# The MLPs' down product: pairs of 256 hidden columns multiplied two at a time in seven products

## The chip, the cores and the metric

One core of a Trainium2 chip runs the whole program in one launch. The metric is the device time of one execution in microseconds. The kernel before took 2644.26 us, the median of three runs (2640.12 to 2646.15).

## What is computed

A trunk of two layers over a sequence of 1024 positions with 1024 channels, in float32. Each layer has a token mixer (a Mamba-2 mixer in layer 0, a gated short convolution in layer 1) and then an MLP. Each sub-layer normalises, scales and shifts by a condition c, and is added back with a gate. The change is in the MLP, where h is 1024 x 1024, `up_w` 1024 x 4096 and `down_w` 4096 x 1024:

```python
def sqrelu_mlp(h, up_w, down_w):
    a = jax.nn.relu(h @ up_w)
    return (a * a) @ down_w
...
        x = x + g_f * sqrelu_mlp(h, mlp_up[i], mlp_down[i])
```

## The kernel before

Activations are kept transposed: `xT[(dt, hf)]` holds 128 channels (dt of 8) by 512 positions (half hf of 2), so a matmul takes 128 x 128 weights and gives 128 x 512 in one PSUM bank. For precision each operand is split in two: a weight tile into hi (cast on ScalarE), lo (raw minus hi, on VectorE) and a bf16 copy (ScalarE), by `split3` (L776), and an activation into ah and al by `keep` (L830). One product of two 128-wide blocks is then three matmuls, hi x ah, lo x ah and bf16 x al, which `mul` (L810) issues into one bank.

`mlp` (L1068) goes over the 4096 hidden columns in 16 pairs of 256. `part_a` and `part_b` (L1016, L1030) make the four blocks of a pair's up product (two blocks of 128 columns by two halves of positions) by seven products of half size (Winograd's form): two in `part_a`, giving c11, and five in `part_b`, giving c12, c22 and c21. In `part_b` GpSimd makes four sums of raw weights (L1036 to L1039) and two of the sums of results (L1052, L1065), and VectorE evicts the other banks (L1050, L1055, L1059, L1063). `relu2` (L1073, its instruction on L1074) squares the ReLU on VectorE. `keep` stores each block in rings of buffers, three for c11 and six for the others.

`do_d` (L1085) is the down product of one pair, by `second` (L840): for each of two halves of the 1024 output channels it loads a raw tile of 512 KB, splits it, and for each of four output tiles and each half of positions runs `mul` over the pair's two blocks, six matmuls into one of four banks tagged "sp". VectorE evicts each bank with the gate into x (L870). A pair is 84 matmuls up and 96 down.

The first two pairs are done apart (`plain_a`, `plain_b`), while the combinations of h are still being made by `combos` (L881) on VectorE, ScalarE and GpSimd. The steady loop then goes, for each i, `do_b(i + 1)`, `do_d(i)`, `do_a(i + 3)`. The last two pairs go through `second` together, with the next stage's work behind each tile.

In layer 0 the down product carries background work: `ada` (L145) makes layer 1's modulation in 48 steps of one 512 KB load and two multiply-adds on VectorE (L160, L162). `do_d` calls one or two steps in each half of the output channels. Raw weights of every kind, ada's among them, share three tiles ("wraw"); hi, lo and bf16 weights have two buffers each.

The order on each engine is made at build time by a scheduler that goes by program order, readiness and priorities; weight splits and GpSimd's sums carry a raised priority. Each engine then runs its own instructions strictly in that order. SyncE issues nearly all loads; GpSimd issues eight small parameter loads at the start (L101 to L116).

## Time and profile before

| | |
|---|---|
| median of three runs | 2644.26 us |
| the profiled execution | 2639.07 us, of which span 2637.4 us |
| TensorE clock granted, mean | 0.98 of full speed |
| busy: TensorE / VectorE / ScalarE / GpSimd | 95% / 77% / 46% / 23% |
| matmuls | 11498 |
| layer 0's MLP, layer 1's MLP | about 860 to 1515 us, 1980 to 2637 us |

An engine counts as busy while an instruction of it is open, also while that instruction itself is held up. A matmul's own duration overlaps the next one's, so their pace is read from counts over a stretch and not from their means.

### The profile page before, as it was taken

The page shows a single profiled execution, that of the slowest core. Times are in us where ns is not written, and L with a number is a line of the kernel's source. Part 1 is how long each engine was busy: PE and PEld are TensorE (multiplying, and loading weights), DVE is VectorE, ACT ScalarE, POOL GpSimd, SP SyncE. Part 2 cuts the span into 40 slices and gives each one's busy share as a digit, 9 for nine tenths or more (in the row PEclk, how much of TensorE's full clock was granted, in tenths as well). Part 3 has the DMA queues.
Part 4 walks back from the last instruction along what each step waited for, and adds up shares of the span by engine and source line. Part 5 has one row for each costly group of instructions (what it writes and reads, how often), then busy time and mean ns, then how long its engine had stood idle before and what let it go on. Part 6 is the DMA issues. An engine that isn't in the chain of part 4 may idle for free. (4 is left out here: it accounts for less than half of the span.)

```text
span 2637.4 us, 31558 instructions
## 1 busy us (share of the span) xinstructions
PE 2503.7 (95%) x11498; PEld 1742.9 (66%) x11498; DVE 2040.8 (77%) x3084; ACT 1226.3 (46%) x2258; POOL 594.3 (23%) x465
## 2 busy tenths in 40 slices
PE   7999999999998799999999998999988999999998
PEld 5777777777776456666666654666544666666666
DVE  7887798887888987878777679765798666666666
ACT  3685565675574524333433345534453343333434
POOL 4221120121121422122222103332234211122120
PEclk9899999999999999999999999999999999999999
DMA  7644443445442233333334122222221221222221
GB/s 226 178 132 132 122 130 107 135 126 150 136 125 61 65 102 105 113 119 111 114 102 120 56 61 75 73 64 70 67 64 48 64 66 55 72 65 64 72 63 74
DMA packets 332412, 256.26 MB, mean 97 GB/s; under 512 B 8824, under 2 KB 289104, under 8 KB 332256
## 3 DMA queue, kind: packets, MB, share of 16 engines
q1 hardware_dynamic: 332000, 254.12, 32.5%
q8 instruction: 90, 1.47, 0.2%
q14 instruction: 66, 0.54, 0.1%
q0 software_dynamic: 256, 0.12, 0.1%
HBM read 249.75 MB, written 4.46 MB: 96 GB/s over the span
## 5 line engine op out<-in xcount | busy, mean ns | idle before, releaser
L870 DVE SCALAR_TENSOR_TENSOR x<-mm,mod,x 128x512 f32<-128x512 f32 (+1 forms) x536 | 387.3, 739 | 136.4 <-PE mm L826 135.2
L826 PEld LDWEIGHTS <-wbf 128*128 128x128 bf16 x2268 | 192.3, 98 | 343.0 <-issue 195.2
L826 PE MATMUL mm<-hh,whi 128*128 128x512 f32 x1196 | 369.0, 427 | 22.5 <-ACT whi L783 9.0
L826 PE MATMUL mm<-ah,wlo 128*128 128x512 f32 (+1 forms) x1072 | 389.9, 427 | 0.0
L826 PE MATMUL mm<-ah,whi 128*128 128x512 f32 (+1 forms) x1072 | 364.4, 431 | 18.5 <-DVE x L870 14.6
L826 PE MATMUL mm<-hh,wlo 128*128 128x512 f32 x1196 | 370.4, 416 | 10.9 <-DVE wlo L784 10.8
L826 PE MATMUL mm<-hl,wbf 128*128 128x512 bf16 x1196 | 318.2, 385 | 4.3 <-ACT wbf L785 4.3
L826 PE MATMUL mm<-al,wbf 128*128 128x512 bf16 (+1 forms) x1072 | 311.6, 382 | 3.7 <-DVE x L870 3.5
L826 PEld LDWEIGHTS mm<-hh,whi 128*128 128x128 f32 x1196 | 230.3, 193 | 71.9 <-ACT hh L956 12.8
L826 PEld LDWEIGHTS mm<-hh,wlo 128*128 128x128 f32 x1196 | 226.9, 190 | 70.2 <-DVE wlo L784 15.7
L208 PE MATMUL mm<-hh,whi 128*128 128x512 f32 x616 | 248.6, 404 | 0.7 <-ACT xs L556 0.7
L210 PE MATMUL mm<-hl,whi 128*128 128x512 f32 x616 | 246.0, 399 | 0.0
L209 PE MATMUL mm<-hh,wlo 128*128 128x512 f32 x616 | 245.4, 398 | 0.3 <-DVE wlo L194 0.3
L826 PEld LDWEIGHTS mm<-ah,whi 128*128 128x128 f32 x1072 | 204.0, 191 | 58.8 <-DVE x L870 17.8
L826 PEld LDWEIGHTS mm<-ah,wlo 128*128 128x128 f32 x1072 | 204.1, 190 | 52.9 <-issue 0.3
L784 DVE TENSOR_TENSOR wlo<-wraw,whi 128x1024 fp32r<-128x1024 f32 x139 | 177.3, 1285 | 66.8 <-ACT whi L783 66.4
L783 ACT CAST whi<-wraw 128x1024 fp32r<-128x1024 f32 x139 | 144.1, 1047 | 129.6 <-PE mm L826 116.3
L785 ACT CAST wbf<-wraw 128x1024 bf16<-128x1024 f32 x139 | 143.7, 1043 | 120.5 <-PE mm L826 116.4
L1036 POOL TENSOR_TENSOR ws<-wraw 128x512 f32<-128x512 f32 x37 | 50.4, 1361 | 493.8 <-DMA wraw<-in_mlp_up_dram 474.5
L208 PEld LDWEIGHTS mm<-hh,whi 128*128 128x128 f32 x616 | 116.5, 189 | 30.6 <-issue 5.8
L210 PEld LDWEIGHTS mm<-hl,whi 128*128 128x128 f32 x616 | 116.5, 189 | 27.3 <-issue 3.7
L209 PEld LDWEIGHTS mm<-hh,wlo 128*128 128x128 f32 x616 | 116.5, 189 | 27.0 <-issue 3.5
(390 smaller groups left out, 4410.6 us busy)
## 6 DMA issues: line engine op xcount, KB each, us to landing
wraw<-in_mlp_up_dram SPq DMA_DIRECT2D x100, 512.0 KB, 3.9
adaw<-in_ada_w_dram SPq DMA_DIRECT2D x96, 512.0 KB, 4.4
wraw<-in_ssd_in_w_dram SPq DMA_DIRECT2D x82, 512.0 KB, 3.9
wdraw<-in_mlp_down_dram SPq DMA_DIRECT2D x64, 512.0 KB, 3.6
wraw<-in_sc_in_w_dram SPq DMA_DIRECT2D x39, 512.0 KB, 3.6
L<-da SPq DMA_DIRECT2D x32, 512.0 KB, 5.0
wdraw<-in_ssd_out_w_dram SPq DMA_DIRECT2D x32, 512.0 KB, 3.4
E<-de SPq DMA_DIRECT2D x56, 128.0 KB, 4.5
```

Source lines behind the costliest of these rows:

```text
L208: PE.matmul(ps, lhsT=hi[:, o:o + P], rhs=ah, start=(k == 0), stop=False)
L209: PE.matmul(ps, lhsT=lo[:, o:o + P], rhs=ah, start=False, stop=False)
L210: PE.matmul(ps, lhsT=hi[:, o:o + P], rhs=al_, start=False, stop=(k == nk - 1))
L783: A.copy(hi[:, :w], raw)
L784: V.tensor_tensor(out=lo[:, :w], in0=raw, in1=hi[:, :w].bitcast(F32), op=ALU.subtract)
L785: A.copy(b[:, :w], raw)
L826: PE.matmul(ps, lhsT=at((hi, lo, b)[j], offs[i]), rhs=blocks[i][j // 2], start=(e == 0), stop=(e == len(js) - 1))
L870: V.scalar_tensor_tensor(out=xv, in0=ps, scalar=g, in1=xv, op0=ALU.mult, op1=ALU.add)
L1036: PL.tensor_tensor(out=s1, in0=a21, in1=a22, op=ALU.add)
```

## The change

Twelve of the sixteen pairs of each MLP (2 to 13) are taken two at a time: their up products, then one `do_w` for both. `do_w` makes the down product of the two pairs for one half of the output channels from seven products, each for two output tiles with two blocks of 128 hidden columns. The seven activation operands of each pair (four blocks and the combinations T1 to T4) are made and kept in `do_b`. Three of the products go through the banks Z: ScalarE reads the bank with the gate applied, GpSimd adds that to x, and the next product is summed into the same bank (`mul` with start=False). The other four end in an eviction by VectorE. Rings of kept activations become one of 14 buffers. To make room in SBUF the program's scratch for GpSimd's own loads is cut to 1024 bytes, and the eight parameter loads at the start go from GpSimd's queue to ScalarE's. The last two pairs and the first two stay as they are.

```diff
-    PL.dma_start(sb[0:96], ssd_conv_w[0].rearrange("k (r p) -> (k r) p", p=P))
+    A.dma_start(sb[0:96], ssd_conv_w[0].rearrange("k (r p) -> (k r) p", p=P))
...
+    def split_to(dst, o, src, pri=200):
+        hi, lo, b = [t[:, o:o + 512].rearrange("p (i n) -> p i n", i=2) for t in dst]
+        with tc.high_priority(offset=pri):
+            A.copy(hi, src)
+            V.tensor_tensor(out=lo, in0=src, in1=hi.bitcast(F32), op=ALU.subtract)
+            A.copy(b, src)
...
-    def keep(tag, r):
-        ah = mp.tile([P, TH], F32R, tag=tag + "h", name=nm("ah"), bufs=dict(a1=3, ab=6)[tag])
-        al_ = mp.tile([P, TH], BF16, tag=tag + "l", name=nm("al"), bufs=dict(a1=3, ab=6)[tag])
+    def keep(r):
+        ah = mp.tile([P, TH], F32R, tag="abh", name=nm("ah"), bufs=14)
+        al_ = mp.tile([P, TH], BF16, tag="abl", name=nm("al"), bufs=14)
...
         def do_a(i):
             c, m1s[i] = part_a(mlp_up[l], i * 256, H)
-            aa[i] = [[keep("a1", relu2(c)), None], [None, None]]
+            cs[i] = relu2(c)
 
         def do_b(i):
-            for (f, hf), c in zip(((0, 1), (1, 1), (1, 0)), part_b(mlp_up[l], i * 256, H, m1s.pop(i))):
-                aa[i][f][hf] = keep("ab", relu2(c))
+            c11 = cs.pop(i)
+            c12, c22, c21 = [relu2(c) for c in part_b(mlp_up[l], i * 256, H, m1s.pop(i))]
+            if i >= n - 2:
+                aa[i] = [[keep(c11), keep(c12)], [keep(c21), keep(c22)]]
+                return
+            b = dict(B11=keep(c11))
+            PL.tensor_tensor(out=c11, in0=c12, in1=c11, op=ALU.subtract)
+            b["B22"] = keep(c22)
+            PL.tensor_tensor(out=c12, in0=c22, in1=c12, op=ALU.subtract)
+            V.tensor_tensor(out=c22, in0=c22, in1=c11, op=ALU.subtract)
+            b["B21"] = keep(c21)
+            V.tensor_tensor(out=c21, in0=c21, in1=c22, op=ALU.subtract)
+            b.update(T1=keep(c11), T2=keep(c22), T3=keep(c12), T4=keep(c21))
+            aa[i] = b
...
+        def do_w(i):
+            ba, bb = aa.pop(i), aa.pop(i + 1)
+            B = {k: [ba[k], bb[k]] for k in ba}
+            w = mlp_down[l]
+            for ds in range(2):
+                raw = [wp.tile([P, 1024], F32, tag="wraw", name=nm("wdraw"), bufs=3) for _ in range(2)]
+                for e in range(2):
+                    SY.dma_start(raw[e].rearrange("p (k n) -> p k n", k=4),
+                                 w[i * 256:i * 256 + 512, ds * 512 + e * 256:ds * 512 + e * 256 + 256].rearrange("(k p) n -> p k n", p=P))
+                (a11, a12), (a21, a22) = [[t.rearrange("p (i h n) -> p h i n", i=2, h=2)[:, h] for h in range(2)] for t in raw]
+                wa = split3(raw[0])
+                s3 = mt("ws", 1)
+                s3v = s3.rearrange("p (i n) -> p i n", i=2)
+                with tc.high_priority(offset=200):
+                    PL.tensor_tensor(out=s3v, in0=a11, in1=a21, op=ALU.subtract)
+                    PL.tensor_tensor(out=a21, in0=a21, in1=a22, op=ALU.add)
+                    PL.tensor_tensor(out=a11, in0=a21, in1=a11, op=ALU.subtract)
+                    PL.tensor_tensor(out=a12, in0=a12, in1=a11, op=ALU.subtract)
...
+                Y = [bank("sp", "dy") for _ in range(2)]
+                Z = [bank("sp", "dz") for _ in range(2)]
...
+                def through(q, ps, g, t):
+                    u = mt(("nt", "acc")[q], 2, tmp)
+                    A.activation(u, ps, AF.Copy, scale=gs[q][g])
+                    PL.tensor_tensor(out=tiles[q][t], in0=tiles[q][t], in1=u, op=ALU.add)
+                def final(q, ps, g, t):
+                    V.scalar_tensor_tensor(out=tiles[q][t], in0=ps, scalar=gs[q][g], in1=tiles[q][t],
+                                           op0=ALU.mult, op1=ALU.add)
+                def step(bk, w3, offs, b, start, end, g, t):
+                    for q in range(2):
+                        mul(bk[q], w3, offs[q], B[b], None, start)
+                        end(q, bk[q], g, t)
...
+                step(Z, wa, wide(0), "B11", True, through, 0, 0)
+                next(bg, None)
+                step(Y, wa, wide(1), "B21", True, final, 0, 0)
+                wb = new3()
+                split_to(wb, 0, a11)
+                split_to(wb, 512, s3v)
+                step(Z, wb, flat(0), "T2", False, through, 1, 2)
+                next(bg, None)
+                W = [bank("sp", "dw") for _ in range(2)]
+                step(W, wb, flat(512), "T3", True, final, 1, 3)
+                wc = split3(raw[1])
+                step(Z, wc, wide(0), "T1", False, through, 1, 3)
+                next(bg, None)
+                step(W, wc, wide(1), "T4", False, final, 1, 2)
+                wd = new3()
+                split_to(wd, 0, a12)
+                step(Z, wd, flat(0), "B22", False, final, 0, 1)
+                next(bg, None)
...
-        do_b(2)
-        do_a(4)
         steady[0], turn_[0] = True, 0
-        for i in range(2, n - 1):
+        for i in range(2, n - 2, 2):
+            do_b(i)
             do_b(i + 1)
-            if i < n - 2:
-                do_d(i)
-                if i + LA < n:
-                    do_a(i + LA)
+            do_a(i + 2)
+            do_a(i + 3)
+            do_w(i)
+        do_b(n - 2)
+        do_b(n - 1)
```

## Rows read from the trace of the kernel before

**Rows 1.** The page: busy time and share of the span of each engine.
```profile
PE 2503.7 (95%) x11498; PEld 1742.9 (66%) x11498; DVE 2040.8 (77%) x3084; ACT 1226.3 (46%) x2258; POOL 594.3 (23%) x465
```
**Rows 2.** Stretches: length; PE, PEld, DVE, ACT, POOL busy us (instructions); clock, DMA, GB/s.
```profile
1043.00:1379.90 336.90, 331.03 (x1473) 223.30 (x1473) 263.81 (x361) 118.89 (x144) 70.81 (x50) 1.00 0.37 113
2114.70:2521.70 407.00, 407.00 (x1801) 275.22 (x1801) 266.22 (x350) 148.67 (x180) 77.58 (x60) 1.00 0.22 65
890.00:930.00 40.00, 28.09 (x98) 16.26 (x97) 38.95 (x35) 19.54 (x27) 28.18 (x17) 0.83 0.18 53
1960.00:2010.00 50.00, 37.52 (x144) 21.11 (x144) 50.00 (x45) 23.80 (x33) 38.68 (x23) 0.93 0.18 53
```
**Rows 3.** Groups by line in layer 1's loop, 2114.7 to 2521.7 (busy us, mean ns).
```profile
L870 DVE SCALAR_TENSOR_TENSOR x<-mm,mod,x 128x512 f32<-128x512 f32 x160 | 117.0, 748 | 48.7 <-PE mm L826 48.5
...
L784 DVE TENSOR_TENSOR wlo<-wraw,whi 128x1024 fp32r<-128x1024 f32 x30 | 36.2, 1221 | 20.1 <-ACT whi L783 20.1
L783 ACT CAST whi<-wraw 128x1024 fp32r<-128x1024 f32 x30 | 31.0, 1048 | 34.1 <-PE mm L826 33.5
...
L834 DVE TENSOR_TENSOR al<-nt,ah 128x512 bf16<-128x512 f32 x20 | 13.7, 686 | 3.4 <-ACT ah L833 3.4
...
L1038 POOL TENSOR_TENSOR wraw<-ws,wraw 128x512 f32<-128x512 f32 x10 | 13.0, 1295 | 0.8
...
L833 ACT CAST ah<-nt 128x512 fp32r<-128x512 f32 x20 | 12.4, 620 | 23.7 <-DVE nt L1074 23.7
L784 DVE TENSOR_TENSOR wlo<-ws,whi 128x512 fp32r<-128x512 f32 x10 | 9.1, 906 | 2.3 <-ACT whi L783 2.2
...
L1022 ACT COPY m<-mm 128x512 f32<-128x512 f32 x10 | 5.9, 587 | 20.2 <-PE mm L826 20.2
```
**Rows 4.** Groups by line in layer 0's loop, 1043.0 to 1379.9.
```profile
L870 DVE SCALAR_TENSOR_TENSOR x<-mm,mod,x 128x512 f32<-128x512 f32 x128 | 92.7, 747 | 19.4 <-PE mm L826 18.9
...
L162 DVE SCALAR_TENSOR_TENSOR adacc<-adaw,cond,adacc 128x512 f32<-128x512 f32 x56 | 44.3, 791 | 4.6 <-DMA adaw<-in_ada_w_dram 4.0
...
L834 DVE TENSOR_TENSOR al<-nt,ah 128x512 bf16<-128x512 f32 x16 | 13.2, 823 | 0.0
...
L784 DVE TENSOR_TENSOR wlo<-ws,whi 128x512 fp32r<-128x512 f32 x8 | 11.2, 1398 | 2.9 <-ACT whi L783 2.9
```
**Rows 5.** Timeline about 1227 us, GpSimd and VectorE (start us, us).
```profile
1226.64 1.68 POOL L1065 TENSOR_TENSOR acc<-t,acc 128x512 f32<-128x512 f32 x1 [4.00 <-DVE t L1059]
...
1227.08 1.80 DVE L834 TENSOR_TENSOR al<-nt,ah 128x512 bf16<-128x512 f32 x1
```
**Rows 6.** Timeline of 905 to 909 us, GpSimd, then VectorE between its starts.
```profile
905.14 1.67 POOL L918 TENSOR_TENSOR nt<-hh,nt 128x512 f32<-128x512 f32 x1 [1.23 <-DVE hl L898]
906.77 1.73 POOL L898 TENSOR_TENSOR hl<-nt,hh 128x512 bf16<-128x512 f32 x1
908.46 1.60 POOL L918 TENSOR_TENSOR nt<-nt,hl 128x512 f32<-128x512 f32 x1
...
905.59 1.76 DVE L1074 SCALAR_TENSOR_TENSOR t<-t 128x512 f32<-128x512 f32 x1
907.28 1.77 DVE L918 TENSOR_TENSOR acc<-acc,hl 128x512 f32<-128x512 f32 x1
```
**Rows 7.** The page's DMA issues: KB each, us from issue to landing.
```profile
wraw<-in_mlp_up_dram SPq DMA_DIRECT2D x100, 512.0 KB, 3.9
adaw<-in_ada_w_dram SPq DMA_DIRECT2D x96, 512.0 KB, 4.4
...
wdraw<-in_mlp_down_dram SPq DMA_DIRECT2D x64, 512.0 KB, 3.6
```
**Rows 8.** Timeline of the start.
```profile
3.11 0.64 SPq L97 DMA_DIRECT2D sa<-in_mix_norm_w_dram  x1
...
5.33 1.06 ACT L404 ACTIVATE xsq<-xin 128x1024 f32<-128x1024 f32 x1 [3.24 <-DMA xin<-in_x_dram]
...
5.56 0.54 POOL L116 DMA_DIRECT2D al<-in_ssd_A_log_dram  x1
```

More of the change, by code (lines that the diff above doesn't have):

```diff
@@ L100, in tile_trunk @@
     sb = xin.tile([P, P], F32, tag="sb", name="sb", bufs=1)
-    PL.dma_start(sb[0:96], ssd_conv_w[0].rearrange("k (r p) -> (k r) p", p=P))
-    PL.dma_start(sb[96:120], rows(ssd_conv_b[0]))
-    PL.dma_start(sb[120:128], rows(final_norm_w))
+    A.dma_start(sb[0:96], ssd_conv_w[0].rearrange("k (r p) -> (k r) p", p=P))
+    A.dma_start(sb[96:120], rows(ssd_conv_b[0]))
+    A.dma_start(sb[120:128], rows(final_norm_w))
     sc_ = xin.tile([P, P], F32, tag="sc", name="scstg", bufs=1)
@@ L110, in tile_trunk @@
                     scalar1=0.5, scalar2=None, op0=ALU.mult)
-    PL.dma_start(sc_[16:32], rows(ssd_norm_w[0]))
-    PL.dma_start(sc_[32:56], sc_conv_w[0].rearrange("k (r p) -> (k r) p", p=P))
+    A.dma_start(sc_[16:32], rows(ssd_norm_w[0]))
+    A.dma_start(sc_[32:56], sc_conv_w[0].rearrange("k (r p) -> (k r) p", p=P))
     params = ((sa, colA), (sb, colB), (sc_, colC))
-    PL.dma_start(dtb, ssd_dt_bias[0].partition_broadcast(P))
+    A.dma_start(dtb, ssd_dt_bias[0].partition_broadcast(P))
     al = xin.tile([P, NH], F32, tag="al", name="al", bufs=1)
-    PL.dma_start(al, ssd_A_log[0].partition_broadcast(P))
+    A.dma_start(al, ssd_A_log[0].partition_broadcast(P))
     A.activation(al, al, AF.Exp)
@@ L808, in tile_trunk, with mul @@
     steady, turn_ = [False], [0]
-    def mul(ps, w, offs, blocks, order=None):
+    def mul(ps, w, offs, blocks, order=None, start=True):
         hi, lo, b = w
@@ L825, in mul @@
         for e, (i, j) in enumerate(js):
-            PE.matmul(ps, lhsT=at((hi, lo, b)[j], offs[i]), rhs=blocks[i][j // 2], start=(e == 0), stop=(e == len(js) - 1))
+            PE.matmul(ps, lhsT=at((hi, lo, b)[j], offs[i]), rhs=blocks[i][j // 2], start=(start and e == 0), stop=(e == len(js) - 1),
+                      skip_group_check=not start)
     LO4, HI4, ALL8 = [[i * P for i in range(*r)] for r in ((0, 4), (4, 8), (0, 8))]
-    def keep(tag, r):
-        ah = mp.tile([P, TH], F32R, tag=tag + "h", name=nm("ah"), bufs=dict(a1=3, ab=6)[tag])
-        al_ = mp.tile([P, TH], BF16, tag=tag + "l", name=nm("al"), bufs=dict(a1=3, ab=6)[tag])
+    def keep(r):
+        ah = mp.tile([P, TH], F32R, tag="abh", name=nm("ah"), bufs=14)
+        al_ = mp.tile([P, TH], BF16, tag="abl", name=nm("al"), bufs=14)
         A.copy(ah, r)
@@ L1088, in do_d, with new3 @@
                     next(bg, None)
+        def do_w(i):
[16 more added lines that the diff above has]
+                    PL.tensor_tensor(out=a12, in0=a12, in1=a11, op=ALU.subtract)
+                tiles = [[xT[(ds * 4 + 2 * e + q, hf)] for e in range(2) for hf in range(2)] for q in range(2)]
+                gs = [[mod[l][:, 40 + ds * 4 + 2 * e + q:41 + ds * 4 + 2 * e + q] for e in range(2)] for q in range(2)]
+                Y = [bank("sp", "dy") for _ in range(2)]
+                Z = [bank("sp", "dz") for _ in range(2)]
+                wide = lambda h: [[j * 512 + h * 256 + q * P for j in range(2)] for q in range(2)]
+                flat = lambda o: [[o + j * 256 + q * P for j in range(2)] for q in range(2)]
+                def through(q, ps, g, t):
[9 more added lines that the diff above has]
+                        end(q, bk[q], g, t)
+                def new3():
+                    return (wp.tile([P, 1024], F32R, tag="whi", name=nm("whi"), bufs=2),
+                            wp.tile([P, 1024], F32R, tag="wlo", name=nm("wlo"), bufs=2),
+                            mp.tile([P, 1024], BF16, tag="wbf", name=nm("wbf"), bufs=2))
+                step(Z, wa, wide(0), "B11", True, through, 0, 0)
[16 more added lines that the diff above has]
+                next(bg, None)
@@ L1095, in mlp @@
             for f in range(2):
-                aa[i][f][0] = keep(("a1", "ab")[f], relu2(half[i][f][0]))
+                aa[i][f][0] = keep(relu2(half[i][f][0]))
         next(more)
@@ L1100, in mlp @@
                 with tc.high_priority(offset=200):
-                    aa[i][f][1] = keep("ab", relu2(c))
+                    aa[i][f][1] = keep(relu2(c))
         do_a(2)
@@ L1168, in unit @@
                 aa.setdefault(ct // 2, [[None, None], [None, None]])[ct % 2][hf] = \
-                    keep("a1" if hf == 0 and ct % 2 == 0 else "ab", o)
+                    keep(o)
         def both(p):
@@ L1193, in out @@
                 V.tensor_tensor(out=r, in0=r, in1=cg[i], op=ALU.mult)
-                aa.setdefault(p, [[None, None], [None, None]])[f][hf] = keep("a1" if i == 0 else "ab", r)
+                aa.setdefault(p, [[None, None], [None, None]])[f][hf] = keep(r)
             r0, m1 = part_a(W, ct * P, H)
```

8 lines of the change are left out of this document (4 added, 4 removed).

## The prediction

> **What bounds the kernel now.** I read the page first, for the share of each engine [rows 1]: TensorE is busy 95% of the span, VectorE 77%, GpSimd 23%. A mean over stages with different limits says little, so next came the busy times of four stretches [rows 2]. The first two are steady stretches of the two MLPs' pair loops. In layer 1 (2114.7 to 2521.7) TensorE is busy all of its 407.0 us: 1801 matmuls, 180 for each of ten pairs, so 40.7 us a pair and 0.226 us a matmul; nothing else binds. In layer 0 (1043.0 to 1379.9) eight pairs take 336.9 us, 42.1 a pair: the work of ada for layer 1 rides on VectorE, which is busy 263.8 us (78%), and TensorE waits a little for evictions. The other two stretches are those before each MLP's loop, where GpSimd is busy 28.2 of 40.0 and 38.7 of 50.0 us; there VectorE is busy the whole time and TensorE is not (28.1 of 40.0 us, clock 0.83). What these two tell of GpSimd and VectorE together decides this case.
>
> I count in **turns**: two pairs, one pass of the new loop. Six turns a layer. A turn takes 81.4 us in layer 1 and 84.2 us in layer 0 now.
>
> **What the change removes.** The down product of two pairs goes from 192 to 168 matmuls (2 column halves x 7 products x 2 output tiles x 6). 24 x 0.226 = 5.4 us a turn, 65 us over twelve turns, if TensorE stays the bound: 76.0 and 78.8 us a turn.
>
> **What it adds, by engine, in a turn.** Prices from layer 1's groups [rows 3].
> VectorE: 16 of 32 evictions go (16 x 0.75 = 12.0 us); six more half-width low parts (6 x 0.69), six more low parts of kept activations (6 x 0.69) and four combinations (4 x 0.69) come: 11.0 us. Its own work stays as it was, 53 us a turn.
> ScalarE: twelve half-width casts (12 x 0.62), twelve reads of a bank (12 x 0.58), six more casts of kept activations (6 x 0.62): 18.1 us on 29.7, so 48 of 76. It has room.
> GpSimd: it had 12 instructions a turn (8 weight sums, 4 for c12 and c22) and gets 36: 8 weight sums for the down product, 4 combinations of activations, 12 additions into x. 36 x 1.30 = 46.8 us of 76, 62% busy where it was 19%.
>
> **What the two share.** In layer 0's loop [rows 4] VectorE's instructions with both inputs in SBUF are longer than in layer 1, where ada's do not press: the half-width low part 1398 ns on average against 906, the low part of nt 823 against 686; those that read PSUM are not (eviction 747 against 748). One case as it happened [rows 5]: GpSimd's addition ran 1226.64 to 1228.32, and VectorE's low part that began at 1227.08 took 1.80 us and ended 0.56 after it; alone it takes 0.69. So an instruction of VectorE with two SBUF inputs and one of GpSimd don't run together; one waits for the other, and its wait counts as busy. Where both always have one waiting [rows 6], GpSimd's starts lie 1.63 and 1.69 us apart with one 512-wide instruction of VectorE between each. Alone the two last 1.30 + 0.69 = 1.99 us; so in such a row they cost 1.69/1.99 = 0.85 of their lone lengths. The steady loops never press on this now: a turn of layer 1 holds 12 x 1.30 + some 25 us of such VectorE work.
>
> [...]
>
> **The sum, half a turn at a time.** Lone lengths x 0.85.
> Up half (two part_b, two part_a, 168 matmuls = 38.0 us of TensorE): GpSimd 16 x 1.30 = 20.8; VectorE with two SBUF inputs, 28 of 512 (2 + 2 x 13: low part, three squared ReLUs, seven kept, two combinations) x 0.69 = 19.3 and 6 of 1024 x 1.22 = 7.3; together 47.4 x 0.85 = 40.3. The half-width low part counts at a kept one's 0.69, since 906 holds waits. Ten evictions that read PSUM (0.69 each, 5.9 in a row) can run while GpSimd holds VectorE's other work up, or not; the trace doesn't show such a mix in steady state, so none to all of it, and I take half: 43.2 us, 5.2 over TensorE.
> Down half (168 matmuls, 38.0): GpSimd 20 x 1.30 = 26.0, VectorE 6 x 0.69 + 4 x 1.22 = 9.0; 35.0 x 0.85 = 29.8, plus half of 16 evictions (10.2): 34.9, under TensorE's 38.0.
> Layer 1: if the up half's lag is made up in the down half a turn is 43.2 + 34.9 = 78.1; if not, 43.2 + 38.0 = 81.2. Kept activations are needed one after another through seven products, so part of the lag carries: 79.6 us, -1.8 on 81.4, x 6 = **-11 us**.
> Layer 0: the down half also calls 8 steps of ada, 16 instructions with two SBUF inputs (791 with their waits; 0.75 alone, as an eviction of the same form; x 0.85 = 10.2): 45.1 us. 43.2 + 45.1 = 88.3 against 84.2: +4.1 a turn. Ada has 48 steps (6 modulations x 2 halves x 4); the first two pairs call 6, so 42 last 5.25 turns: **+21 us**; the rest, at layer 1's 79.6 against 84.2, x 0.75 = **-3**.
> Weight buffers: the seventh product has only 12 matmuls (2.7 us) to cover the next weights' cast and low part (1.05 + 1.22 = 2.3 us alone), and behind a GpSimd instruction it is late by about half a microsecond, in twelve turns **+6** (0 to 20). ScalarE's cast that waits for such a buffer holds the bank reads queued behind it, and product 3 writes the bank that they free; 18 matmuls (4.1 us) lie between.
> SP's queue issues four loads of down weights a turn as now, in pieces of 1 KB for 2; those of the up weights, with 512-byte pieces, land in 3.9 us against 3.6, so nothing by itself [rows 7]. Raw tiles: one pool of three holds the down weights and, in layer 0, ada's. The first raw tile is held through six products and the second through four; 3.6 landing + 4 x 1.30 of sums + some 14 and 8 us of products, 23 + 17; ada's four take 4.4 to land and 1.5 to use, 24. 64 over three tiles is 21 us for a half of 19. Where the next half's tiles come late, GpSimd's sums, the casts and product 3 come late in turn. I take half of the 2 us, in 10.5 halves: **+10** (0 to 50).
> Finals: the second product's eviction reads the x tile that GpSimd has just added to, so VectorE waits with all behind it if GpSimd is late; ScalarE's read and GpSimd's addition (0.58 + 1.30) have a product's 2.7 us. Nothing, up to 1 us a half (+24).
> The start: eight parameter loads move from GpSimd's queue to ScalarE's [rows 8]. ScalarE is idle for 3.2 us before its first Square at 5.33; eight issues at SP's price there (0.64) are 5.1, so its first Square may start some 2 us late, with little to gain on GpSimd, whose eight end at 6.1. I take nothing, -1 to +3. More buffers for kept activations (14 for 9) also serve the short convolution: layer 1's TensorE waits for none of them in its loop, and the convolution's waits are in no row here: I take nothing, 0 to -5.
> Sum: -11 + 21 - 3 + 6 + 10 = **+23 us**. The profiled execution took 2639.07 (2637.4 of span and 1.7 around it), so 2662; the median of the runs is 5.2 higher, and set on it the sum is 2667. I say **2667**.
>
> **Rivals.** *TensorE stays the bound.* If the evictions all run while GpSimd works and the lag is carried, layer 1 gets its 76.0 and layer 0 its port's 80.3 (47.4 + 35.0 + 12.0, x 0.85): -5.4 x 6 - 3.9 x 5.25 - 5.4 x 0.75 = -57, or 2587; with the 16 us of buffers 2603. For it: a TensorE that waits for nothing in layer 1, and VectorE busy only 65% there. Against it: the 62% of GpSimd. Chance 0.35.
> *The lock costs its whole length.* Pairs at 1.99: 82.4 us a turn in layer 1 and 94.4 in layer 0, +1.0 x 6 + 10.2 x 5.25 = +60, or 2704, with buffers 2720. For it: the single case in rows 5; against it: the 1.69 of rows 6. It is decided by whether both engines keep one waiting. [...] Chance 0.15.
> *Raw tiles decide layer 0.* Ada's loads take the third tile before each half's own: 5 us in each of 10.5 halves in place of my 1, +42 on the forecast: 2709. It decides only while ada runs; layer 1 would show none of it. Chance 0.12.
> That the matmuls don't go is no rival: their count is fixed, 288 fewer.
>
> **How the numbers follow.** The forecast has the remaining 0.38; its own range is 2630 to 2695. 0.2%, 5.3 us, is about what a measurement of this kernel can tell from no change. Of the forecast's share about 0.09 lies within that and 0.03 below; of the first rival's 0.01 within. Faster 0.37, same 0.10, slower 0.53. The range leaves a quarter of the first rival below (2600) and the worst of the other two above (2725).
>
> **What would show it.** Right: GpSimd near 60% in both loops, VectorE above 90% in layer 0's, its two-input instructions at 0.9 us and more where they were 0.69, TensorE's waits in the loops on low parts and evictions, layer 0's turn longer than 84, layer 1's near 80. Wrong: layer 1's loop with TensorE busy throughout at 76 us a turn (first rival), or waits on landings of down weights in layer 0 (third).

## The result, and the profile after

The changed kernel took **2803.9 us**, the median of four runs (2799.0 to 2807.5), against 2644.6 for the kernel before (four runs): a ratio of 1.0604, interval 1.0583 to 1.0625. I had said 2667, and up to 2725.

The page, first line: busy time and share of the span of each engine (before: [rows 1]).

```profile
PE 2505.2 (89%) x11210; PEld 1705.5 (61%) x11210; DVE 2174.8 (78%) x3084; ACT 1422.4 (51%) x2618; POOL 1036.2 (37%) x745
```

The 288 matmuls are gone, yet TensorE is busy as long as before and its share fell from 95% to 89%: it waits, and it runs slower. Where is read from two stretches, five turns of layer 0's loop with ada and the six turns of layer 1's (columns as in [rows 2]):

```profile
994.60:1506.00 511.40, 420.62 (x1719) 264.75 (x1718) 394.92 (x453) 229.34 (x332) 273.62 (x180) 0.96 0.31 93
2162.10:2708.90 546.80, 479.85 (x2018) 309.62 (x2017) 376.58 (x421) 277.25 (x397) 319.03 (x216) 0.98 0.19 58
```

A turn (I measure it between every second copy of an up product's first bank by ScalarE, `A.copy(m5, p1)` in `part_b`) takes 546.8 / 6 = **91.1 us** in layer 1, where it was 81.4, and 511.4 / 5 = **102.3** in layer 0, where it was 84.1. That is 6 x 9.7 + 5.25 x 18.2 = 154 of the 159 us.

336 matmuls a turn by 0.226 us are 75.9 us [rows 2]. In layer 1 TensorE is idle for 11.2 us of a turn and busy for 80.0 (479.85 / 6), 4.1 more than 75.9. Of these 4.1 the granted clock explains about 1.8: 0.98 of full speed over 546.8 us is 10.9 us lost in six turns. The other 2.3 are not split up by any run. An estimate for part of them: TensorE waited 46 times in the six turns, and if the last matmul before each wait shows its whole length, some 0.40 us by the means below where one starts every 0.226, that is 46 x 0.17 / 6 = 1.3 a turn. In layer 0 it is busy 84.1 and idle 18.2, and the clock of 0.96 explains about 4.1. The waits, TensorE's groups by line in layer 1's stretch (busy us, mean ns | idle before, and who ended it):

```profile
L834 PE MATMUL mm<-hh,wlo 128*128 128x512 f32 x338 | 102.2, 424 | 17.0 <-DVE wlo L784 17.0
L834 PE MATMUL mm<-hh,whi 128*128 128x512 f32 x336 | 90.3, 402 | 19.6 <-ACT acc L1054 10.1 <-DVE nt L1072 8.3 <-ACT whi L783 1.2
L834 PE MATMUL mm<-hl,wbf 128*128 128x512 bf16 x336 | 80.9, 381 | 8.2 <-ACT wbf L785 8.2
L834 PE MATMUL dz<-ah,wlo 128*128 128x512 f32 x192 | 73.1, 462 | 20.7 <-DVE wlo L784 12.6 <-DVE wlo L793 7.8
```

In layer 1's loop before, TensorE waited for nothing [rows 2]. Of the 67.0 us now, more than half (17.0 + 20.7) are for low parts of weights, VectorE's work; 18.4 are for banks of the up product that ScalarE or VectorE has not read yet. In layer 0, where most of the time is lost, the 90.8 us of waits in five turns are spread wider. The four largest (us in total, times, longest):

```profile
PE adaps L168 <- DVE adacc L162: 16.8, 10, 2.8
PE dz L834 <- DVE wlo L793: 14.5, 5, 2.9
PE mm L834 <- ACT wbf L785: 12.2, 5, 2.5
PE dw L834 <- DVE x L1145: 9.4, 6, 1.9
```

Low parts of weights are about 27 of the 90.8 there. The first line is ada's: its multiply-adds on VectorE took 1161 ns where they took 791 [rows 4].

```profile
L162 DVE SCALAR_TENSOR_TENSOR adacc<-adaw,cond,adacc 128x512 f32<-128x512 f32 x70 | 81.3, 1161 | 6.2 <-DMA adaw<-in_ada_w_dram 5.1
```

VectorE's groups in layer 1's stretch, to be held against [rows 3]:

```profile
L784 DVE TENSOR_TENSOR wlo<-wraw,whi 128x1024 fp32r<-128x1024 f32 x37 | 44.6, 1218 | 20.5 <-issue 19.8 <-ACT whi L783 0.7
...
L1145 DVE SCALAR_TENSOR_TENSOR x<-dw,mod,x 128x512 f32<-128x512 f32 x48 | 35.8, 750 | 60.6 <-PE dw L834 60.6
L843 DVE TENSOR_TENSOR al<-nt,ah 128x512 bf16<-128x512 f32 x36 | 31.3, 895 | 1.0
L843 DVE TENSOR_TENSOR al<-acc,ah 128x512 bf16<-128x512 f32 x24 | 26.7, 1115 | 4.1 <-ACT ah L842 4.1
L793 DVE TENSOR_TENSOR wlo<-wdraw,whi 128x512 fp32r<-128x512 f32 x24 | 26.7, 1113 | 2.5 <-ACT whi L792 1.8
```

Two things are to be seen. Many instructions with two SBUF inputs are stretched (a kept low part 895 and 1115 ns for 686, a half-width weight low part 1113; not the low part of an up weight, 1218 for 1221), evictions from PSUM are not (750). And VectorE is far from full, 69% here and 77% in layer 0; it stood idle 60.6 us in front of evictions, waiting for TensorE, in the very stretch in which TensorE waited 37.7 us for its low parts. Idle time in front of evictions is no loss by itself, since the old loop had 48.7 us of it in five turns [rows 3] while TensorE never waited. It shows that VectorE had time, only not where a low part was wanted. That the fixed order of each engine keeps the two from making up for each other is my reading; no run changes that alone.

One such place, the timeline of layer 1 at 2380 to 2386 us (start, length), TensorE, VectorE, GpSimd:

```profile
2381.94 0.62 PE L834 MATMUL dz<-ah,whi 128*128 128x512 f32 x2
2384.95 0.93 PE L834 MATMUL dz<-ah,wlo 128*128 128x512 f32 x2 [2.39 <-DVE wlo L784]
2385.68 1.93 PE L834 MATMUL dz<-al,wbf 128*128 128x512 bf16 x4
...
2381.24 1.45 DVE L843 TENSOR_TENSOR al<-acc,ah 128x512 bf16<-128x512 f32 x1
2382.61 2.28 DVE L784 TENSOR_TENSOR wlo<-wdraw,whi 128x1024 fp32r<-128x1024 f32 x1
...
2380.84 1.30 POOL L1127 TENSOR_TENSOR ws<-wdraw,wdraw 128x512 f32<-128x512 f32 x1 [5.85 <-DVE al L843]
2382.22 1.59 POOL L1128 TENSOR_TENSOR wdraw<-wdraw 128x512 f32<-128x512 f32 x1
```

GpSimd's two sums of weights hold up first a kept low part (1.45 us for 0.69), then the first product's weight low part (2.28 for 1.22): 1.8 us late together, and TensorE stands for 2.39. Then it runs slower: its granted clock in the 4 us that follow (columns as above),

```profile
2379.00:2382.50 3.50, 3.50 (x16) 2.27 (x14) 3.42 (x5) 3.50 (x7) 1.58 (x2) 1.00 0.34 118
2385.00:2389.00 4.00, 4.00 (x11) 2.32 (x12) 4.00 (x4) 2.25 (x4) 3.23 (x3) 0.57 0.01 2
```

was 0.57 of full speed, where it was 1.00 before the wait: 11 matmuls in 4 us instead of some 17. If that is the wait's doing, which no run shows, the late low part is paid for again here: 4 x (1 - 0.57) = 1.7 us behind a wait of 2.39. Not every wait is followed by this. Behind one of 2.33 us at the same place two turns earlier the clock was 1.00:

```profile
2204.93 0.73 PE L834 MATMUL dz<-ah,wlo 128*128 128x512 f32 x2 [2.33 <-DVE wlo L784]
...
2205.00:2209.00 4.00, 4.00 (x19) 2.47 (x19) 4.00 (x4) 2.36 (x5) 3.26 (x3) 1.00 0.00 0
```

### The profile page after: what moved, and what is told of

It reads as the page before. It is cut to its first block, busy times and chain, and to the rows that moved or that the text cites. A ratio compares the mean times of both kernels' runs of the same rounds, so it can differ in the third digit from the quotient of the medians.

```text
span 2801.8 us, 32047 instructions
## 1 busy us (share of the span) xinstructions
PE 2505.2 (89%) x11210; PEld 1705.5 (61%) x11210; DVE 2174.8 (78%) x3084; ACT 1422.4 (51%) x2618; POOL 1036.2 (37%) x745
## 5 line engine op out<-in xcount | busy, mean ns | idle before, releaser
L834 PE MATMUL mm<-hh,whi 128*128 128x512 f32 x1196 | 379.3, 433 | 63.8 <-ACT acc L1054 20.1
L834 PE MATMUL mm<-hh,wlo 128*128 128x512 f32 x1196 | 379.8, 424 | 36.7 <-DVE wlo L784 36.3
L834 PEld LDWEIGHTS <-wbf 128*128 128x128 bf16 x2172 | 186.6, 99 | 353.6 <-issue 194.3
L208 PE MATMUL mm<-hh,whi 128*128 128x512 f32 x616 | 248.7, 404 | 0.5 <-ACT xs L556 0.5
L209 PE MATMUL mm<-hh,wlo 128*128 128x512 f32 x616 | 245.1, 398 | 0.9 <-DVE wlo L194 0.9
L834 PE MATMUL dz<-ah,wlo 128*128 128x512 f32 x384 | 149.0, 470 | 46.5 <-DVE wlo L793 25.1
L1142 POOL TENSOR_TENSOR x<-x,nt 128x512 f32<-128x512 f32 x72 | 112.1, 1557 | 142.5 <-ACT nt L1141 131.3
L834 PE MATMUL mm<-ah,whi 128*128 128x512 f32 (+1 forms) x304 | 150.7, 520 | 10.0 <-DVE x L879 7.2
L162 DVE SCALAR_TENSOR_TENSOR adacc<-adaw,cond,adacc 128x512 f32<-128x512 f32 x140 | 141.0, 1007 | 8.0 <-DMA adaw<-in_ada_w_dram 6.4
L879 DVE SCALAR_TENSOR_TENSOR x<-mm,mod,x 128x512 f32<-128x512 f32 (+1 forms) x152 | 107.2, 718 | 42.6 <-PE mm L834 42.2
L666 POOL TENSOR_TENSOR xs<-xs,yo 128x512 f32<-128x512 f32 x28 | 45.2, 1614 | 245.7 <-DVE xs L663 216.0
L834 PE MATMUL dz<-ah,whi 128*128 128x512 f32 x384 | 123.6, 409 | 7.9 <-ACT nt L1141 4.4
```

The source lines that it names most:

```text
L162: V.scalar_tensor_tensor(out=acc, in0=wv, scalar=cond[:, kt:kt + 1], in1=acc, op0=ALU.mult, op1=ALU.add)
L208: PE.matmul(ps, lhsT=hi[:, o:o + P], rhs=ah, start=(k == 0), stop=False)
L209: PE.matmul(ps, lhsT=lo[:, o:o + P], rhs=ah, start=False, stop=False)
L666: PL.tensor_tensor(out=xs[:, :, cs], in0=xs[:, :, cs], in1=t, op=ALU.add)
L834: PE.matmul(ps, lhsT=at((hi, lo, b)[j], offs[i]), rhs=blocks[i][j // 2], start=(start and e == 0), stop=(e == len(js) - 1), skip_group_che ...
L879: V.scalar_tensor_tensor(out=xv, in0=ps, scalar=g, in1=xv, op0=ALU.mult, op1=ALU.add)
```

## The experiments

Each ran once, with a profile, beside the kernel before on the same chip; those runs of it lie between 2635.7 and 2644.2, so the comparisons rest on turns (us; six of layer 1, the five with ada of layer 0; of the old loop the first is left out). In the changed kernel with four raw tiles, the low parts of one set of combinations of h (T4's in the MLPs, T3's in the convolution) are left out to make room, and T2's stand in for them; in the loops only the tiles differ. no_added_gpsimd, no_added_gpsimd_4raw, no_weight_sums and sums_aside leave sums out of the result and so compute another product; they are read for their times only.

| kernel | total | before | layer 1 | layer 0 |
|---|---|---|---|---|
| before | | | 81.4 | 84.1 |
| changed | 2803.9 | 2644.6 | 91.1 | 102.3 |
| no_added_gpsimd | 2667.9 | 2635.7 | 82.9 | 87.2 |
| no_weight_sums | 2727.7 | 2641.5 | 86.3 | 94.2 |
| additions_on_vectore | 2789.2 | 2641.5 | 90.9 | 100.8 |
| four_raw_tiles | 2733.2 | 2635.7 | 86.7 | 94.5 |
| no_added_gpsimd_4raw | 2604.6 | 2643.4 | 78.6 | 80.7 |
| additions_on_vectore_4raw | 2717.8 | 2643.4 | 86.6 | 92.4 |
| sums_aside | 2799.2 | 2644.2 | 92.6 | 99.0 |
| sums_on_vectore_4raw | 2691.7 | 2644.2 | 82.7 | 92.6 |
| before_more_gpsimd | 2728.4 | 2641.5 | 85.0 | 95.5 |
| before_gpsimd_fills | 2654.0 | 2635.7 | 83.3 | 85.1 |
| order_only | 2689.4 | 2641.5 | 85.1 | 87.5 |
| parts_spread | 2838.3 | 2635.7 | 91.9 | 106.3 |
| before_more_buffers | 2684.7 | 2643.4 | 86.8 | 83.1 |
| layer1_only_4raw | 2677.3 | 2643.4 | 85.1 | old |
| layer1_only_sums_v | 2648.8 | 2644.2 | 82.8 | old |
| layer1_sums_additions_v | 2660.9 | 2638.3 | 83.9 | old |
| layer1_nothing_on_gpsimd | 2657.6 | 2638.3 | 83.8 | old |

### How much is GpSimd's added work, and which part of it

**no_added_gpsimd**: all 24 added GpSimd instructions of a turn left out.

```diff
-            PL.tensor_tensor(out=c11, in0=c12, in1=c11, op=ALU.subtract)
-            PL.tensor_tensor(out=c12, in0=c22, in1=c12, op=ALU.subtract)
...
-                    PL.tensor_tensor(out=s3v, in0=a11, in1=a21, op=ALU.subtract)
...
-                    PL.tensor_tensor(out=tiles[q][t], in0=tiles[q][t], in1=u, op=ALU.add)
```

> All 24 GpSimd instructions that the change adds in a turn are left out: the weight sums, the additions into x (ScalarE still reads the banks, and nobody takes the result) and the two subtractions for T1 and T3. GpSimd is back at 12 a turn; the seven products, their weights' casts and the seven kept activations stay. Lock theory: TensorE's 76 us plus what the order costs in the run of the order alone (3.8 and 3.4): layer 1 near 80, layer 0 near 83 (VectorE's own work in 78.8), total 2600 to 2640. If the ring of banks, the weight buffers of the last product or the seven kept activations are what holds it, layer 1 stays at 84 or more even so.

**no_weight_sums**: only the four sums of weights in each half left out (the lines from `s3v` on).

> GpSimd's four sums of raw down weights in each half are left out (the raw quarters are used as they are, so the down product of these pairs is another one): 8 GpSimd instructions fewer in a turn and a chain of 4 fewer between a raw tile's landing and its casts. Lock theory: about 9 us less a turn, layer 1 near 83, layer 0 near 94, total near 2705. Chain theory: the waits of the down products' own weights go (about 16 of the 55 us that TensorE waits in five turns of layer 1, so 3 a turn, and what the clock loses behind them), those of the up product stay: layer 1 near 87, layer 0 near 97, total 2740 to 2760.

**additions_on_vectore**: the finished sums go into x by an eviction on VectorE.

```diff
-                    A.activation(u, ps, AF.Copy, scale=gs[q][g])
-                    PL.tensor_tensor(out=tiles[q][t], in0=tiles[q][t], in1=u, op=ALU.add)
+                    V.scalar_tensor_tensor(out=tiles[q][t], in0=ps, scalar=gs[q][g], in1=tiles[q][t],
+                                           op0=ALU.mult, op1=ALU.add)
```

> The three products whose banks ScalarE read and GpSimd added to x are now evicted by VectorE straight from the bank, as the other four: a turn loses 12 GpSimd additions and 12 ScalarE reads, and VectorE gets 12 evictions (0.75 us each). A turn takes about 91 us in layer 1 and 102 in layer 0 in the changed kernel. Lock theory (each GpSimd instruction holds VectorE's two-input work up for about 1.1 us, and VectorE then holds TensorE up): about 13 us less of that a turn, minus 9 us of evictions that don't meet the lock, so layer 1 near 84 and layer 0 near 92, total near 2705. Chain theory (TensorE waits for links that run in order: raw tile, GpSimd's sums, casts, low part, and bank reads behind casts; the additions at a chain's end don't matter): within 3 us a turn, total 2770 to 2840.

The added work is worth 91.1 - 82.9 = 8.2 us a turn in layer 1 and 102.3 - 87.2 = 15.1 in layer 0. The weight sums make more than half of it (4.8 and 8.1). Without them layer 1 came out near the chain theory's 87 (86.3), layer 0 at the lock theory's 94 (94.2). Moving the twelve additions, GpSimd's largest part, to VectorE wins only 0.2 and 1.5. That is not what they cost: VectorE gets twelve evictions in exchange, and TensorE now waits for these in layer 1's six turns, where in the changed kernel it waited 1.5 us for ScalarE's reads of the same banks:

```profile
PE dz L834 <- DVE x L1140: 10.6, 4, 3.4
```

What the additions cost on GpSimd stays open; with T1 and T3 they are what the weight sums leave, 3.4 and 7.0. Even with no added GpSimd work the seven products still lose: 82.9 and 87.2 us a turn, more than the 80 and 83 that the lock theory expected.

### The raw tiles

**four_raw_tiles**: one more buffer of raw weights.

```diff
-        raw = wp.tile([P, 1024], F32, tag="wraw", name=nm("wraw"), bufs=3)
+        raw = wp.tile([P, 1024], F32, tag="wraw", name=nm("wraw"), bufs=4)
```

> The changed kernel with four raw weight tiles for three. To make room the low parts of one set of combinations of h are left out (T4's in the MLPs, T3's in the convolution, T2's stand in), which changes nothing in the loops' instructions; the two loops alone are compared, at 91.2 and 102.0 us a turn with three tiles. Raw-tile rival (up weights and ada's land late because the down products hold two of three tiles): layer 0 to 95 or less, layer 1 to 88 or less. Lock theory: GpSimd and VectorE do the same work, so within 1.5 us of 91.2 and 102.0.

**no_added_gpsimd_4raw**: both edits.

> The run without the 24 added GpSimd instructions (82.9 and 86.7 us a turn), with four raw tiles for three as before (the low parts of one set of combinations of h left out). If two causes, GpSimd's exclusion of VectorE and the late raw tiles, hold the change and nothing else, a turn comes near TensorE's 76.0 and 78.8: layer 1 at 76 to 79, layer 0 at 79 to 82, total 2575 to 2620. If the banks, the weight buffers or the seven kept activations hold it too, layer 1 stays at 81 or more and layer 0 at 84 or more.

**additions_on_vectore_4raw**: four tiles, and the additions on VectorE.

> The changed kernel with four raw tiles (86.2 and 94.5 us a turn) and with the twelve additions moved from ScalarE and GpSimd to VectorE's evictions. With three tiles the move gave 0.3 and 1.3 us a turn. Lock theory: the late raw tiles hid it, and it shows now: 3 or more a turn, layer 1 to 83, layer 0 to 91, total 2690 to 2705. Chain theory: the additions are at a chain's end, so within 1 us a turn, total 2720 to 2740.

The fourth tile gives 4.4 us a turn in layer 1 and 7.8 in layer 0; with GpSimd's added work gone it gives 4.3 and 6.5. With four tiles, moving the additions wins 0.1 and 2.1, again less than the lock theory's 3 or more. So there are **two causes that nearly add up**. Layer 1: 75.9 of matmuls + 2.7 left over + 4.3 tiles + 8.2 GpSimd = 91.1. Layer 0: 80.7 + 6.5 + 15.1 = 102.3. TensorE's groups in layer 1 of no_added_gpsimd_4raw show the waits nearly gone:

```profile
L834 PE MATMUL mm<-hh,wlo 128*128 128x512 f32 x338 | 101.0, 420 | 0.5 <-DVE wlo L784 0.2
L834 PE MATMUL mm<-hh,whi 128*128 128x512 f32 x336 | 86.5, 394 | 6.8 <-ACT acc L1063 6.8
...
L834 PE MATMUL dz<-ah,wlo 128*128 128x512 f32 x192 | 69.2, 441 | 3.3 <-DVE wlo L784 3.3
```

That the tiles bind in layer 1 as well was not expected. SyncE's queue hints at how: what its loads of up weights (L812) waited for in layer 1's stretch of the changed kernel (total us, times, longest),

```profile
SPq L812 <- DVE wlo L784: 288.1, 30, 16.6
```

and in that of four_raw_tiles:

```profile
SPq L812 <- DVE wlo L784: 230.8, 24, 14.7
```

The loads wait until VectorE has made a low part and so freed a tile, 48.0 us a turn with three tiles and 38.5 with four. Such waits are no cost in themselves. In layer 1's loop of the old kernel (five turns) they were 40.9 a turn, and TensorE waited for nothing:

```profile
SPq L804 <- DVE wlo L784: 204.7, 30, 10.2
```

That the tiles bind is shown by the turns, 91.1 and 86.7; that they do so through low parts that come late behind GpSimd's sums fits these waits, but no run shows it alone.

### Is it the lock between GpSimd and VectorE

The next four runs ask whether GpSimd's work costs because VectorE's instructions with two SBUF inputs wait for it (the lock, as the expectations call it; [rows 5] has one case, 1.80 us for 0.69), or because the sums stand in the row from landed weights to casts and low parts.

**before_more_gpsimd**: the old kernel, with 24 GpSimd instructions a turn that read two SBUF inputs and whose result nobody reads.

```diff
+        if steady[0] and inmlp[0]:
+            for _ in range(2):
+                PL.tensor_tensor(out=scr[0], in0=ah.bitcast(F32), in1=ah.bitcast(F32), op=ALU.subtract)
...
+                        PL.tensor_tensor(out=scr[0], in0=xv, in1=xv, op=ALU.subtract)
```

> The kernel before with 24 GpSimd additions more in each two pairs (36 as in the changed kernel), into a scratch tile that nobody reads: two after each kept activation, one after four of the evictions. Nothing waits for their results, so this is the lock alone. Lock theory by the forecast's prices: layer 1 between 81.4 and 84 us for two pairs, since VectorE has room there, and layer 0 at 88 to 92, total 2665 to 2705. Chain theory: VectorE's instructions get longer but TensorE hardly waits, under 1 us for two pairs, total 2640 to 2655.

**before_gpsimd_fills**: the same places, but each of the 24 is replaced by three fills, which read nothing (with one copy of a single column at each place, so that they come no earlier).

```diff
+        PL.tensor_copy(scr[0][:, 0:1], v.bitcast(F32)[:, 0:1])
+        for _ in range(3 * k):
+            PL.memset(scr[0], 0.0)
```

> The kernel before with the 24 added GpSimd additions in two pairs replaced by fills that read nothing: for each, three fills of the same 128x512 scratch tile with zeros (and a copy of one column that ties them to the same moment). If it is reading from SBUF by both engines that excludes them (lock theory): near 2645, two pairs at 81.4 and 84 to 86. If any use of GpSimd does it (its writes, or its mere being busy): layer 0 at 90 or more, total 2680 or more.

Layer 0's loop of before_more_gpsimd (columns as above), and two of TensorE's groups there:

```profile
1054.50:1532.20 477.70, 430.92 (x1806) 290.55 (x1840) 367.02 (x447) 148.23 (x182) 240.46 (x181) 0.95 0.32 97
```

```profile
L827 PE MATMUL mm<-ah,whi 128*128 128x512 f32 x320 | 98.2, 424 | 29.8 <-DVE x L874 29.8
L827 PE MATMUL mm<-al,wbf 128*128 128x512 bf16 x300 | 87.4, 406 | 16.1 <-DVE x L874 14.7
```

and layer 0's loop of before_gpsimd_fills:

```profile
1054.50:1480.00 425.50, 417.03 (x1847) 280.33 (x1846) 328.34 (x448) 148.17 (x182) 306.18 (x500) 1.00 0.36 109
```

Work that nobody waits for cost the old kernel 11.4 us a turn in layer 0 and 3.6 in layer 1, while VectorE was busy 77% and 70% of the time. In layer 0 evictions still took 745 ns, but stood behind stretched instructions; TensorE waited for them 44.5 us in five turns, and its clock was 0.95. With fills GpSimd was busy longer there (72% of the stretch, not 50%), yet a turn cost only 1.0 us more. A kept low part took 1306 ns on average in layer 0's loop with the additions and 681 with the fills:

```profile
L835 DVE TENSOR_TENSOR al<-nt,ah 128x512 bf16<-128x512 f32 x20 | 26.1, 1306 | 0.0
...
L841 DVE TENSOR_TENSOR al<-nt,ah 128x512 bf16<-128x512 f32 x20 | 13.6, 681 | 0.0
```

So in layer 0 it isn't GpSimd's time that costs, but its reading beside VectorE. In layer 1 this test is less clear, since the fills cost 1.9 of the 3.6 us. There VectorE waited in five turns for GpSimd's own sums of results, first in the old loop, then with fills:

```profile
DVE acc L1074 <- POOL acc L1065: 14.8, 10, 1.5
...
DVE acc L1085 <- POOL acc L1076: 24.8, 10, 2.5
DVE nt L1066 <- POOL nt L1063: 10.4, 5, 2.1
```

So about half of that cost may be GpSimd's longer queue and not its reading.

**sums_aside**: the changed kernel, the eight weight sums at their places but on kept activations, into scratch.

```diff
-                    PL.tensor_tensor(out=s3v, in0=a11, in1=a21, op=ALU.subtract)
...
+                    for v in (B["B11"][0], B["B11"][1], B["B22"][0], B["B22"][1]):
+                        PL.tensor_tensor(out=s3, in0=v[0].bitcast(F32), in1=v[0].bitcast(F32), op=ALU.subtract)
```

> The changed kernel with its eight GpSimd sums of weights in a pair of halves left at their places, of the same size and type, but taken from kept activations into scratch tiles that nobody reads; the products read the unsummed weights, so the weight sums are left out of the result. Theory of the lock (the sums cost because GpSimd works beside VectorE): turns of layer 1 about 91 us and of layer 0 about 101, total about 2800. Theory of the chain (they cost because the landed raw tile, the sums, the casts and the low parts stand in a row): turns of 86.3 and 94, as without the sums, total about 2728. Rival: both have a share, then 88 to 89 and 97 to 98, total about 2765.

**sums_on_vectore_4raw**: four raw tiles, the eight sums on VectorE (PL becomes V in the same lines).

> The change with four raw tiles (so the low parts of the half activations left out, as in the run four_raw_tiles), the eight sums of weights in a turn on VectorE. If the lock is what the sums cost: VectorE has 5.5 us more a turn (8 sums of 0.69) but 4.9 (layer 1) and 7.8 (layer 0) of stalls go: turns of about 83 to 85 and 88 to 91, total about 2670 to 2690. If the chain is what they cost: no gain over four_raw_tiles, 86 and 94 or more, total 2733 or more.

With the sums out of the row, layer 1's turn is 92.6: all that leaving them out had won (to 86.3) is lost again. In layer 0 it is 99.0, so of 8.1 us 4.8 come back and 3.3 belong to the row. GpSimd also waited some 7 us a turn in layer 1 for the kept activation that it reads, so its queue is a rival. But VectorE and ScalarE waited no longer for what GpSimd makes than in no_weight_sums (39.5 and 97.7 us in six turns, there 42.8 and 97.6), while the low part of an up weight, which has two SBUF inputs, took 1492 ns where it took 1218 in no_weight_sums and in the changed kernel:

```profile
L784 DVE TENSOR_TENSOR wlo<-wraw,whi 128x1024 fp32r<-128x1024 f32 x37 | 54.7, 1492 | 20.4 <-issue 19.8 <-ACT whi L783 0.7
```

The other way round, VectorE takes some 6.5 us a turn of sums more and the turn gets shorter: 86.7 to 82.7, and 94.5 to 92.6. (This shortens the row too, as a sum takes about 0.8 us there and 1.5 on GpSimd, so it can't tell the two apart alone.) The first run says **the lock** in layer 1, and more lock than row in layer 0; the second agrees.

### The order of the work, and buffers

**order_only**: the changed kernel's loop and rings of 14, with the old down products.

```diff
-            do_w(i)
+            do_d(i)
+            do_d(i + 1)
```

> The order and the rings of the changed kernel (two up products, two first parts, then the down products, 14 buffers of kept activations) with the down products of before (192 matmuls, no combinations, no bank reads by ScalarE). GpSimd is back at 12 instructions a turn. Lock theory: as before, 81.4 and 84.2 us a turn, total 2640 to 2660. Order theory (the rival: two up products in a row bunch the kept activations and the casts, and TensorE waits for their evictions): layer 1 at 84 or more, total 2680 or more.

**parts_spread**: the up parts alternate.

```diff
             do_b(i)
-            do_b(i + 1)
             do_a(i + 2)
+            do_b(i + 1)
             do_a(i + 3)
```

> The changed kernel with the two first parts put between and behind the two five-product parts (b, a, b, a in place of b, b, a, a), nothing else. Order theory (in the run of the order alone a turn took 85.2 and 87.4 for 81.4 and 84.0, TensorE waiting for low parts of weights in the second part_b, while the first one's kept activations stand ahead on ScalarE and VectorE): about the 3.8 and 3.4 us a turn come back, total 2755 to 2775. Lock theory: the same instructions, so within 1 us a turn, total 2790 to 2815.

**before_more_buffers**: the old kernel with four raw tiles, three buffers each of hi, lo and bf16 weights, and the start's loads on ScalarE's queue.

> The kernel before with the room that the change makes (loads at the start on ScalarE's queue, small scratch) given to a fourth raw tile and a third buffer of hi, lo and bf16 weights, nothing else. If layer 0's 2.6 us for two pairs above layer 1 come from late raw tiles or weights, 82 for 84 and some in the other stages: 2610 to 2632. If VectorE's late evictions cause it, as the waits of the profile before say: 2632 to 2646.

Two pairs' up parts in a row, with old down products, cost 3.7 and 3.4 us a turn by themselves, with three raw tiles: in layer 1 TensorE then waits 11.5 us in six turns for low parts of up weights (that their loads and sums now come bunched is my reading, not shown). Spreading them is no cure: neither theory's total came, and layer 0 gets worse by 4.0. And more buffers made the old kernel slower in layer 1, 86.8 for 81.4: in 407 us of its loop TensorE waited 17.3 us for evictions, where the kernel before has no wait:

```profile
L826 PE MATMUL mm<-ah,whi 128*128 128x512 f32 x301 | 86.1, 403 | 7.0 <-DVE x L870 7.0
L826 PE MATMUL mm<-al,wbf 128*128 128x512 bf16 x302 | 81.2, 387 | 10.3 <-DVE x L870 10.3
```

More freedom to split weights early changes the order in which the scheduler lines up VectorE's work; that this is why evictions come late there is argued, not shown.

### Is there a version that gains

**layer1_only_4raw**: layer 0 keeps its old products; four tiles; additions, T1 and T3 on VectorE.

> The seven products in layer 1's MLP alone, with four raw tiles, the additions and the combinations T1 and T3 on VectorE (20 GpSimd instructions a turn for 36); layer 0's MLP in the order and with the products of before. It beats the kernel before if layer 1's turn is under 81.4. Lock theory: from 86.2 with 16 GpSimd instructions fewer 81 to 83, total 2630 to 2655. Chain theory: 85 to 87, total 2655 to 2680.

**layer1_only_sums_v**: its additions back on ScalarE and GpSimd, its weight sums on VectorE.

> Seven products in layer 1 alone, four raw tiles, all sums and differences of weights and activations on VectorE, none on GpSimd; the additions of the finished sums on ScalarE and GpSimd. Against the run layer1_only_4raw (turns of 85.0): if the lock by the sums is what is left, turns of 80 to 82 and a total of about 2640 to 2655, which is no slower than the kernel before; if VectorE's own length decides, 84 to 87 and 2670 to 2690. Layer 0 keeps its old products in both, at about 83 us a turn.

**layer1_sums_additions_v** and **layer1_nothing_on_gpsimd**: the sums and the additions on VectorE; T1 and T3 on GpSimd in the first, on VectorE in the second.

> As layer1_only_sums_v, but the additions of the finished sums are done by VectorE too and the two differences T1 and T3 by GpSimd, so that GpSimd has 4 added instructions in a turn for 12. If GpSimd's additions still cost by the lock, turns of layer 1 of 80 to 82 and a total of 2632 to 2644, below the kernel before. If VectorE's length decides (12 evictions of 0.75 more, 9 us a turn), 83 to 86 and 2650 to 2668.

> As layer1_sums_additions_v, with T1 and T3 on VectorE as well: none of the 24 added instructions of a turn is GpSimd's. If the lock is still what holds it, faster than that run, 79 to 81 a turn and 2626 to 2640; if VectorE's length decides, slower by some 1 to 2 us a turn, 84 to 88, 2656 to 2680.

None is faster than the kernel before. The best, layer1_only_sums_v, comes to 2648.8 beside 2644.2 (82.8 us a turn), a difference that one run each can't tell from none, and it leaves low parts out. Taking more off GpSimd brings nothing more: 83.9 and 83.8, and the wait has a new place, here in the last of them (TensorE's groups, layer 1):

```profile
L834 PE MATMUL dz<-ah,whi 128*128 128x512 f32 x192 | 60.6, 403 | 16.2 <-DVE x L1153 16.2
```

The bank Z, which ScalarE read in the change, is now freed by VectorE, and behind its other work. Only no_added_gpsimd_4raw (2604.6, 39 us below the one before) shows a gain, of the 65 us that 288 matmuls by 0.226 come to; it leaves all the added sums and additions out and is no kernel to use.

## Why the prediction was wrong

**What is removed** held: 288 matmuls, and 336 x 0.226 = 75.9 us a turn is what TensorE needs. The first rival's 76.0 and 2587 to 2603 were nearly reached, 78.6 and 2604.6, but only with GpSimd's added work and the third-tile limit both taken away.

**What two instructions share** was seen rightly: beside more GpSimd work many of VectorE's instructions with two SBUF inputs took longer (a kept low part 895 and 1115 ns for 686 in layer 1), evictions did not (750 ns there, 747 and 748 before), and GpSimd was 58% busy in layer 1 and 54% in layer 0 (62% foretold). The waits fell on low parts for more than half in layer 1, but for less than a third in layer 0. No run shows a lock or a port as such, the prediction's words for what the two engines share. What is shown are these stretched lengths and, before the change, GpSimd's starts 1.63 and 1.69 us apart with one VectorE instruction between each [rows 6]; where the first rival has its port's 80.3 us, layer 0's turn took 102.3, and 80.7 with both causes gone.

**The sum, half a turn at a time**, is the step that failed. It took the pair of engines for one resource with a throughput: lone lengths x 0.85, compared with 38.0 us of TensorE, what is over counted, what is under hidden. It made 79.6 and 88.3 a turn. VectorE would then be over 90% busy in layer 0; it was 77%, as full as in the old loop. No engine was full. At the place shown above, two instructions of VectorE that stood 0.8 and 1.1 us behind GpSimd's made a low part late, and TensorE waited for that one. Nor was the lag made up in the easier half. In layer 1's six turns the up products waited 44.8 us (17.0 + 19.6 + 8.2), 7.5 a turn, where the sum had their half 5.2 over. The down products, where it had 3.1 to spare (38.0 - 34.9), waited 20.7, 3.5 a turn, for low parts. (The raw tiles have a share in both.) The lower clock, 1.8 us a turn there, had no term. Added GpSimd work cost 8.2 and 15.1 us a turn where my sums had (over TensorE's length) 79.6 - 76.0 = 3.6 and 88.3 - 78.8 = 9.5: about 28 + 29 = 57 us too little in all, less the 6 of the next term.

**Weight buffers, +6**: "late by about half a microsecond, in twelve turns". At the place meant, the product right behind a seventh one, TensorE hardly waited in the turn of layer 1 that begins at 2162 us: 0.18 us for the second half's first product, and nothing for the first up product of the next turn.

```profile
2226.58 0.74 PE L834 MATMUL dz<-ah,wlo 128*128 128x512 f32 x2 [0.18 <-DVE wlo L784]
```

Waits for low parts of weights lay elsewhere; they were 37.7 us in layer 1's six turns, 6.3 a turn, part of the above.

**Raw tiles, +10**, in layer 0 alone: they cost 4.3 x 6 + 6.5 x 5.25 = 60 us. The rival "Raw tiles decide layer 0" had 5 us a half, so 10 a turn there, nearer than the forecast, but "layer 1 would show none of it" is refuted: 4.3 us a turn, with no ada at all. I had counted how long tiles are held against three tiles with ada's four loads in the half, and left out that the up weights share the three tiles in both layers, where a tile is held until a low part that may itself come late.

**The order** has no term in the sum, and the prediction gives no reason for that. 2.7 a turn in layer 1 and 80.7 - 78.8 = 1.9 in layer 0 remain with both causes gone, 26 us. That this is the order is argued from order_only, whose 3.7 and 3.4 were measured with three tiles. These three misses, some 51 + 50 + 26 = 127 us, are most of the 137 between 2667 and 2803.9.

**The lock's whole length** would have given 82.4 and 94.4 us, and 2720: also far short of 91.1 and 102.3, for the same reason, since it too is a sum of lengths.

**Finals and start** were right. VectorE's eviction of the second product waited 3.7 us in layer 1's six turns for GpSimd's addition, 0.6 a turn, within the "up to 1 us a half":

```profile
L1145 DVE SCALAR_TENSOR_TENSOR x<-dy,mod,x 128x512 f32<-128x512 f32 x24 | 17.4, 741 | 3.7 <-POOL x L1142 3.7
```

The first Square began at 5.66 for 5.33 [rows 8], behind eight issues on ScalarE's queue that ended at 4.33. The loads with other pieces landed as fast, 3.5 us for down weights [rows 7]:

```profile
wdraw<-in_mlp_down_dram SPq DMA_DIRECT2D x64, 512.0 KB, 3.5
```

## What to carry to other kernels

When TensorE is fed by engines with fixed orders, don't ask whether a helper has room on average; ask for each thing that TensorE waits for by how much it may be late, and count a lower clock as well (0.57 over the 4 us behind one wait of 2.39 us here, 1.00 behind one of 2.33). Work given to GpSimd that reads SBUF was paid here by VectorE's two-input instructions (a kept low part in layer 0's old loop 1306 ns, beside fills 681) and whoever waits for them, even where nobody waits for GpSimd; try it first by adding such work, unused, to the old kernel, which here cost 87 us at once. And saving matmuls by sums of operands would be worth its price only where the sums have an engine and buffers that the feeding of TensorE doesn't need; no run here found such a place.
